# Decoder layer on one core: the last group's residual rows spaced, the order of two products in the gate and up blocks exchanged, and GpSimd's sums of weights held until the first group's residual is there

## The chip, the cores and the metric

The kernel runs on one core of one Trainium2 chip. The metric is the device time of one execution in microseconds (us). Of the kernel before, three runs gave 2595.02, 2599.94 and 2601.57 us; their median, 2599.94 us, is the time before.

## The reference

One layer of a hybrid decoder over 2048 tokens of 1024 numbers, in float32. The FFN is 2816 wide.

```python
a = _rmsnorm(h, g_pre_mix);  u = a @ w_in
conv_out = _conformer_conv(c_val, c_gate, ...)      # GLU, causal depthwise conv of width 31, LayerNorm, swish
attn_out = _rmsnorm(_stick_breaking(q, k, v), attn_norm_g)
y = concat([conv_out, attn_out]) @ w_out
h = h + _rmsnorm(y, g_post_mix)
f_in = _rmsnorm(h, g_pre_ffn)
f = (silu(f_in @ w_gate) * (f_in @ w_up)) @ w_down
h = h + _rmsnorm(f, g_post_ffn)
```

The attention has 8 heads of 64; for each query its weights are products of sigmoids that run backwards over the keys, so that a running product (a scan) stands where a softmax usually does.

## The kernel before, in words

The 2048 tokens are four groups of 512 (`NG`, `G`). Every float32 operand is split into a high part, rounded to TensorE's fp32r, and the low rest; a product is then three matmuls (high by low, high by high, low by high). ScalarE (ACT) writes the high part, VectorE (DVE) or GpSimd (POOL) subtracts to get the low one.

**Up to the last output projection** the order is set by a table, `PLAN` (L39): for each group the input projection ("in"), the convolution's and the attention's halves of the output projection ("outc", "outa"), then for groups 0 and 2 the first FFN products ("c11", "p4"). Three generators run beside it: `attn` (attention), `taps` (the convolution on DVE) and `sums` (L834). How far each may be advanced at a position of the table is a list of points: `ATTN`, `TAPS` and `SUMS` (L71: nothing before position 330, all by position 900). What these lists fix is the order in which the program is written. The framework then orders the instructions of each engine by readiness under a timeline of its own, so an instruction whose inputs and buffers are free can be placed far ahead of where it was written.

**The sums of weights.** The FFN products are done by a scheme of fast matrix multiplication on two by two blocks: it needs, besides the weights, sums and differences of their quarters. `sums` builds 132 of them on POOL (L844, `combine`), 88 from w_gate and w_up and 44 from w_down: each takes a load of 256 KB into one of three rotating tiles with the tag `sum`, one POOL operation on 128x512 numbers and a store of 256 KB (L772 for those of w_gate and w_up, two to a tensor, the pairs named (6, 5) and (7, 3); L766 for w_down). They are read again only in the FFN. In the attention POOL has other work: `om` (the running product, a DVE scan, L572) is multiplied into the weights `A` by POOL (L573), TensorE transposes `A` (L589, `at`), and goes on.

**The gate and up blocks** (`five`, L1106). After the last output projection there are 44 blocks: for the two FFN row groups g = 0 and g = 2 (each pairs two groups of 512 tokens), for each of 11 column blocks j, one block with the gate weights (i = 0) and one with the up weights (i = 1). A block is made of products numbered 3 to 7, of 12 matmuls each. Product 6 of the next block goes into a fresh bank `b2`; DVE reads it (`second`, L1131; u2 = b2 + s1); product 7 is added to the same bank and DVE reads that (u3 = b2 + s1); product 5 goes into a fresh bank `b3`, DVE adds it (u3 = b3 + u3), then product 3 is added to `b3` and read (b3 + u2). A product that adds to a bank has to wait until DVE has read what stood there. For g = 0 product 4 was computed earlier ("p4"), so a block is four products; for g = 2 it is five. The order of TensorE's products and of these DVE operations is pinned to the order of writing (`keep_in_program_order`). Per block TensorE runs product 5, product 7, product 6 of the next block, product 3. `hidden` (L1082) follows each up block: four DVE operations between tiles in on-chip memory (s1, s2, a difference, s4) make the operands of the down projection from the four results.

The operands of the blocks of g = 2 are themselves sums of quarters, made by `input_sums` (L886), which needs the normed residual rows of the last group. Those are made beside the first blocks: `steps` (L1197) takes `residual_parts` (L712) of four tiles of 128 rows, in two parts each, and then `input_sums`; one step is taken per block, or two in every second one from block 5 on (`todo`, L1216). A tile's residual is: a load of x, a square on ACT with a sum, a power on POOL (`rs`), a scaling on DVE (L722), two additions on POOL (L725), a store, a second square and power (`rstd2`), a scaling on ACT (L730). The load of x and the squares' output use tiles with the tag `row`, four of them, which the blocks use as well for their weights (`raw2`) and results (`a22`).

The splits of a block's weights into high and low parts are L1064 (ACT) and L1065 (POOL). After the blocks comes the down projection (`dps`).

## Time and profile before

The profiled execution of the kernel before took 2596.21 us by the device's clock; its span, from the first to the last instruction, is 2594.5 us.

| stretch of the span (us) | what runs | TensorE (PE) busy | DVE busy | POOL busy | GB/s |
|---|---|---|---|---|---|
| 0 to 430 | input projections, attention and convolution of the first groups | 388.41 | 327.25 | 281.86 | 297 |
| 430 to 1050 | the same of later groups, first FFN products | 576.07 | 532.90 | 399.95 | 305 |
| 1050 to 1450 | FFN products and attention of the last group | 392.38 | 248.87 | 197.16 | 237 |
| 1450 to 1542 | end of the attention, last output projection | 78.16 | 43.13 | 22.85 | 143 |
| 1542 to 1842 | gate and up blocks, g = 0 | 269.96 | 194.23 | 179.30 | 258 |
| 1842 to 2143 | gate and up blocks, g = 2 | 299.43 | 175.53 | 125.89 | 195 |
| 2143 to 2594 | down projection and the end | 430.18 | 266.72 | 266.10 | 214 |

A busy time is the time in which an engine has an instruction running, in this one execution; what is missing to the stretch's length is idle. GB/s is what all transfers moved. In rows of instructions, "out<-in" names tiles; the number behind the bar is the mean of one in ns; in rows of a timeline the square bracket gives the engine's idle time before the instruction and what ended it. In rows of waits the three numbers are the total in us, the count and the longest. Tiles of the blocks keep the names of the buffers that they reuse: u2 and u3 are written to `glu`, `cy` and `cs`; the operand of product 3 is `e__17579`, that of product 7 `e__17561`; `b` is a bank.

### The profile page before, as it was taken

What the parts mean: (1) busy time and instruction counts of PE and PEld (TensorE: products, weight loads), DVE (VectorE), ACT (ScalarE), POOL (GpSimd) and SP (SyncE); (2) the same over time, 40 slices, a digit from 0 to 9 for tenths busy, and PEclk for the clock granted to TensorE, in tenths of its full rate; (3) what the DMA queues carried; (4) which work ended last, traced back from release to release, by engine and by line L of the source; (5) the groups of instructions that cost most, each with busy time, mean ns of one, the idle gap of its engine ahead of it and who ended that gap; (6) DMA issues with size and microseconds to landing.
All of it is one profiled execution on the core that took longest, in us unless ns stands there. A gap on an engine that the chain in (4) does not pass through costs nothing. (4 is left out here: it accounts for less than half of the span.)

```text
span 2594.5 us, 35632 instructions
## 1 busy us (share of the span) xinstructions
PE 2434.6 (94%) x11156; PEld 1963.6 (76%) x11156; DVE 1788.6 (69%) x2321; ACT 1292.8 (50%) x2398; POOL 1473.1 (57%) x1844
## 2 busy tenths in 40 slices
PE   7989989998999999999999988899999999999997
PEld 6877767776777777887788766777777777887886
DVE  5797589958996898876544545766555655557556
ACT  4555555555555656667756734332332233453543
POOL 5764678556755777559433226764443444567556
PEclk9999999999999999999999989999999999999999
DMA  9989888988898898747977636986656557668655
GB/s 341 326 302 310 287 260 279 348 268 284 286 314 272 321 345 280 270 152 235 306 247 235 221 108 220 323 291 223 199 190 201 192 197 262 193 192 283 206 189 174
DMA packets 289182, 657.31 MB, mean 253 GB/s; under 512 B 33889, under 2 KB 42081, under 8 KB 288993
## 3 DMA queue, kind: packets, MB, share of 16 engines
q1 hardware_dynamic: 264704, 622.01, 71.6%
q10 hardware_dynamic: 24288, 33.04, 3.5%
q8 instruction: 88, 1.44, 0.2%
q14 instruction: 102, 0.83, 0.1%
HBM read 460.92 MB, written 193.99 MB: 252 GB/s over the span
## 5 line engine op out<-in xcount | busy, mean ns | idle before, releaser
L573 POOL TENSOR_TENSOR A<-A,om 128x512 f32<-128x512 f32 (+2 forms) x320 | 312.6, 977 | 410.0 <-DVE om L572 372.0
L572 DVE TENSOR_TENSOR_SCAN om<-om,one,z 128x513 f32<-128x513 f32 (+2 forms) x320 | 351.7, 1114 | 110.0 <-ACT A L570 104.5
L1065 POOL TENSOR_TENSOR wL<-raw,wH 128x512 fp32r<-128x512 f32 x176 | 248.9, 1441 | 286.5 <-issue 158.2
L476 DVE SCALAR_TENSOR_TENSOR cv<-glu,cw,cv 128x512 f32<-128x512 f32 x464 | 347.4, 749 | 6.7
L1245 DVE TENSOR_TENSOR xL__21999<-t__22001,xH__21998 128x512 fp32r<-128x512 f32 x154 | 199.1, 1301 | 159.6 <-ACT xH__21998 L1244 159.4
L1243 POOL TENSOR_TENSOR xL__21997<-t__22000,xH__21996 128x512 fp32r<-128x512 f32 x154 | 207.6, 1353 | 175.0 <-ACT xH__21996 L1242 174.5
L256 PE MATMUL inps<-xH,wL 128*128 128x512 f32 x640 | 260.8, 408 | 11.3 <-ACT sg L422 10.3
L249 DVE TENSOR_TENSOR TL<-at,TH 128x512 fp32r<-128x512 f32 (+1 forms) x320 | 188.8, 600 | 112.0 <-ACT TH L248 111.6
L260 PE MATMUL inps<-xL,wH 128*128 128x512 f32 x640 | 258.6, 405 | 0.2 <-DVE xL L392 0.2
L258 PE MATMUL inps<-xH,wH 128*128 128x512 f32 x640 | 258.2, 404 | 0.0
L760 PE MATMUL dps<-xH__21996,xL__21999 128*128 128x512 f32 x616 | 240.9, 391 | 8.1 <-DVE xL__21999 L1245 7.2
L568 ACT ACTIVATE om<-z 128x512 f32<-128x512 f32 (+2 forms) x320 | 171.6, 539 | 153.5 <-PE z L563 70.6
L760 PE MATMUL dps<-xL__21997,xH__21998 128*128 128x512 f32 x616 | 240.8, 391 | 2.0 <-POOL xL__21997 L1243 2.0
L760 PE MATMUL dps<-xH__21996,xH__21998 128*128 128x512 f32 x616 | 240.5, 390 | 0.0
L844 POOL TENSOR_TENSOR sum<-sum 128x512 f32<-128x512 f32 x132 | 172.6, 1308 | 84.8 <-DMA sum<-in_w_up_dram 28.5
L248 ACT ACTIVATE TH<-at 128x512 fp32r<-128x512 f32 (+1 forms) x320 | 168.0, 547 | 103.2 <-PE at L589 94.0
L1242 ACT ACTIVATE xH__21996<-t__22000 128x512 fp32r<-128x512 f32 x154 | 97.2, 631 | 233.0 <-POOL xL__21997 L1243 148.7
L589 PE MATMUL at<-idr,A 128*128 128x128 f32 x1088 | 191.4, 280 | 7.5 <-POOL A L573 5.6
L210 ACT ACTIVATE wH<-raw 128x1024 fp32r<-128x1024 f32 x156 | 165.6, 1064 | 65.0 <-DMA raw<-in_w_in_dram 29.6
L1064 ACT ACTIVATE wH<-raw 128x512 fp32r<-128x512 f32 x176 | 101.1, 623 | 165.0 <-PE b L760 76.4
L570 ACT ACTIVATE A<-z 128x512 f32<-128x512 f32 (+2 forms) x320 | 168.6, 542 | 19.2 <-PE at L589 14.4
L589 PEld LDWEIGHTS at<-idr,A 128*128 128x128 f32 x1088 | 142.2, 144 | 43.9 <-POOL A L573 6.8
(294 smaller groups left out, 6225.8 us busy)
## 6 DMA issues: line engine op xcount, KB each, us to landing
wL<-wL SPq DMA_DIRECT2D x156, 512.0 KB, 5.1
raw<-in_w_in_dram SPq DMA_DIRECT2D x80, 512.0 KB, 6.4
t__22001<-u SPq DMA_DIRECT2D x154, 256.0 KB, 2.8
c<-c ACTq DMA_DIRECT2D x88, 256.0 KB, 4.4
t__22000<-wd SPq DMA_DIRECT2D x88, 256.0 KB, 2.9
K<-kd SPq DMA_DIRECT2D x80, 256.0 KB, 4.7
V<-vd SPq DMA_DIRECT2D x80, 256.0 KB, 4.7
u<-accf SPq DMA_DIRECT2D x22, 768.0 KB, 4.1
```

Of the source, the lines that this page charges most:

```text
L249: nc.vector.tensor_tensor(L, ps, H.bitcast(F32), ALU.subtract)
L256: nc.tensor.matmul(ps, WL[:, kc], aH[t](k), start=k == 0, stop=False)
L258: nc.tensor.matmul(ps, WH[:, kc], aH[t](k), start=False, stop=False)
L260: nc.tensor.matmul(ps, WH[:, kc], aL[t](k), start=False, stop=k == KT - 1)
L476: nc.vector.scalar_tensor_tensor(to, gl[c][:, k:k + G], cw[:, c, k:k + 1], a, ALU.mult, ALU.add))
L572: nc.vector.tensor_tensor_scan(r, r, z[:, 0:1].to_broadcast([P, w + 1]), one, ALU.mult, ALU.bypass)
L573: nc.gpsimd.tensor_tensor(a[:, 0:w], a[:, 0:w], om[:, G - w + 1:G + 1], ALU.mult)
L589: nc.tensor.transpose(pt[:, j * P:(j + 1) * P], u["A"][j][:, b * P:(b + 1) * P], id32)
L760: return nc.tensor.matmul(ps, a, b, skip_group_check=True, **flags)
L1065: nc.gpsimd.tensor_tensor(l, t, f32(h), sub)
L1243: nc.gpsimd.tensor_tensor(WL, w, f32(WH), sub)
L1245: nc.vector.tensor_tensor(UL, t, f32(UH), sub)
```

## The change

**The sums of weights.** `SUMS` starts at position 414 of the table and ends at 930. In `sums`, three tiles with the tag `sum` are taken first and one number in each is set on POOL; then POOL adds to each a number of `rstd2[:, 3:4]`, which is made by the residual of the last tile of group 0. The real sums need the same three buffers, so none of their loads can be issued before that. The pairs stored together are now (6, 7) and (5, 3).

**The order of products.** Product 7 of a block now comes first and product 5 second. The second half of `hidden` is written between the two DVE operations on u3; its stores are queued in two portions.

**The residual of the last group.** The rows of x are loaded into four half tiles that are free at that time (`e[2:4]`), no longer into `row`; the squares' output goes to another small tile. A tile's residual has four parts instead of two, and the parts of a tile are written one block apart. `steps` has two steps more, and block 16 takes two.

```diff
-SUMS = ((330, 0.0), (900, 1.0))
+SUMS = ((414, 0.0), (415, 0.002), (930, 1.0))
...
-        r, junk = row("xr"), row("junk")
...
+        yield
         nc.sync.dma_start(hd[T], y)
         rms_of(rstd2[:, T:T + 1], y, junk)
         done.add(("h", T))
+        yield
...
+        held = [fup.tile([P, G], F32, tag="sum", name="held", bufs=3) for _ in range(3)]
+        for t in held:
+            nc.gpsimd.memset(t[:, 0:1], 0.0)
+        yield 0
+        for t in held:
+            nc.gpsimd.tensor_tensor(sp.tile([P, 1], F32, tag="held", name="h"), t[:, 0:1], rstd2[:, 3:4], add)
...
             dve(s1, a21, a22, add)
             dve(s2, s1, a11, sub)
+            for n, t in ((1, a11), (4, a22)):
+                late.append([1, t, "u", g, n, j])
+            yield
             dve(a21, a21, a11, sub)
             dve(s4, a12, s2, sub)
...
                 b3 = gu("b3")
-                b.mul(b3, 5, True)
+                b.mul(b.b2, 7, False)
                 nxt = Block(n + 1) if n + 1 < NB else None
                 for fn, *args in behind:
                     fn(*args)
                 c11 = result(b.i, (1, 1), b.c11)
-                b.mul(b.b2, 7, False)
+                b.mul(b3, 5, True)
                 u3 = next(u_)
                 dve(u3, b.b2, b.s1, add)
                 p4_ = b.A.get("p4")
                 if p4_ is not None:
                     dve(p4_, u3, p4_, add)
+                if more_h:
+                    next(more_h.pop())
                 dve(u3, b3, u3, add)
...
-            parts = [residual_parts((NG - 1) * TT + t, True) for t in range(TT)]
-            for t in range(TT + 1):
-                for p in parts[max(t - 1, 0):t + 1][::-1]:
+            xr = [m[:, i:i + 2, :].rearrange("p a t -> p (a t)") for m in operand(*e[2:4], dt=F32) for i in (0, 2)]
+            parts = [residual_parts((NG - 1) * TT + t, xr[t], keep=True) for t in range(TT)]
+            for t in range(TT + 3):
+                for p in parts[max(t - 3, 0):t + 1]:
                     next(p)
                 yield
...
-        todo = {n: [(next, more)] * (1 if n < 5 else 2 - n % 2) for n in range(16)}
+        todo = {n: [(next, more)] * (1 if n < 5 else 2 - n % 2) for n in range(17)}
```

POOL's order near the start of the program, before: `raw` and `wL` are weights of the first input projection, `sum` the sums of weights.

```order
L214 TENSOR_TENSOR wL_332<-raw_333,wH_331 128x1024
L844 TENSOR_TENSOR sum_5465<-sum_5463,sum_5465 128x512
L844 TENSOR_TENSOR sum_5463<-sum_5463,sum_5467 128x512
L844 TENSOR_TENSOR sum_5467<-sum_5465,sum_5467 128x512
L214 TENSOR_TENSOR wL_340<-raw_341,wH_339 128x1024
```

The first sums now, on the same engine, right behind the held tiles' additions and among the attention's operations (`A` is multiplied at L573, `rstd2` made at L192):

```order
L192 TENSOR_TENSOR rstd2_76<-ms_6498,nhalf_73 128x1
L192 TENSOR_TENSOR rstd1_75<-ms_7080,nhalf_73 128x1
L191 TENSOR_SCALAR ms_7188<-ss_7186 128x1
L848 TENSOR_TENSOR h_8140<-held_8134,rstd2_76 128x1
L848 TENSOR_TENSOR h_8142<-held_8135,rstd2_76 128x1
L192 TENSOR_TENSOR rstd1_75<-ms_7188,nhalf_73 128x1
L848 TENSOR_TENSOR h_8144<-held_8136,rstd2_76 128x1
L573 TENSOR_TENSOR A_4740<-A_4740,om_4737 128x512
```

The 132 sums have moved as a whole: before, the first stood ahead of POOL's first product `A` and the last behind the 208th of 320; now the first stands behind the 90th and the last behind the 298th, and 81 of them stand ahead of the 211th.

DVE's order at one gate block of g = 0 that follows an up block, before: from the read of product 3 (`b3` and u2) over the multiplication by the up result, the four operations of `hidden`, to the two reads of u3 with the addition to `a22` between them, and the read of the next product 6.

```order
L1072 TENSOR_TENSOR b3_18711<-b3_18711,cy_17518 128x512
L1072 TENSOR_TENSOR lng_117<-b3_18711,lng_117 128x512
L1072 TENSOR_TENSOR accf_17520<-lng_117,sumf_17523 128x512
L1072 TENSOR_TENSOR accf_17520<-accf_17520,sumf_17522 128x512
L1072 TENSOR_TENSOR lng_117<-lng_117,sumf_17522 128x512
L1072 TENSOR_TENSOR accf_17520<-sumf_17524,accf_17520 128x512
L1072 TENSOR_TENSOR cy_17518<-b2_18774,glu0_132 128x512
L1072 TENSOR_TENSOR a22_18726<-cy_17518,a22_18726 128x512
L1072 TENSOR_TENSOR cy_17518<-b3_18810,cy_17518 128x512
L1072 TENSOR_TENSOR cs_17519<-b2_18863,glu1_134 128x512
```

The same place now:

```order
L1080 TENSOR_TENSOR b3_18713<-b3_18713,cy_17530 128x512
L1080 TENSOR_TENSOR lng_117<-b3_18713,lng_117 128x512
L1080 TENSOR_TENSOR accf_17532<-lng_117,sumf_17535 128x512
L1080 TENSOR_TENSOR accf_17532<-accf_17532,sumf_17534 128x512
L1080 TENSOR_TENSOR cy_17530<-b2_18769,glu0_132 128x512
L1080 TENSOR_TENSOR a22_18728<-cy_17530,a22_18728 128x512
L1080 TENSOR_TENSOR lng_117<-lng_117,sumf_17534 128x512
L1080 TENSOR_TENSOR accf_17532<-sumf_17536,accf_17532 128x512
L1080 TENSOR_TENSOR cy_17530<-b3_18805,cy_17530 128x512
L1080 TENSOR_TENSOR cs_17531<-b2_18857,glu1_134 128x512
```

The first read of u3 and the addition to `a22` have moved ahead of the last two operations of `hidden`; the number of operations between the read of product 3 and the second read of u3 is the same.

DVE's order at the start of the blocks, before (`glu3` takes u2 of block 0, `cy` u3 of block 0):

```order
L1072 TENSOR_TENSOR glu3_138<-b2_17617,glu0_132 128x512
L1072 TENSOR_TENSOR cy_17518<-b2_17617,glu0_132 128x512
L1072 TENSOR_TENSOR a22_17597<-cy_17518,a22_17597 128x512
L1072 TENSOR_TENSOR cy_17518<-b3_17631,cy_17518 128x512
L1072 TENSOR_TENSOR cs_17519<-b2_17674,glu1_134 128x512
```

And now:

```order
L1080 TENSOR_TENSOR glu3_138<-b2_17629,glu0_132 128x512
L722 SCALAR_TENSOR_TENSOR big_17215<-big_17215,rs_17748,gain_17745 128x1024
L722 SCALAR_TENSOR_TENSOR big_17215<-big_17215,rs_17840,gain_17745 128x1024
L1080 TENSOR_TENSOR cy_17530<-b2_17629,glu0_132 128x512
L1080 TENSOR_TENSOR a22_17609<-cy_17530,a22_17609 128x512
L1080 TENSOR_TENSOR cy_17530<-b3_17643,cy_17530 128x512
L1080 TENSOR_TENSOR cs_17531<-b2_17686,glu1_134 128x512
```

The residual's scaling of tiles 0 and 1 (L722) has moved ahead of u3 of block 0; the scaling of tiles 2 and 3 stands between blocks 0 and 1, where before the four were spread up to block 4. So the order that the framework made draws the residual together, though it is written further apart. The transposes of the last group's rows, which begin after product 16 of the blocks before, begin after product 7.

More of the change, by code (lines that the diff above doesn't have):

```diff
@@ L705, in layer_kernel, with residual, residual_parts @@
     gpo = []
-    def residual(T, keep=False):
-        for _ in residual_parts(T, keep):
+    def residual(T):
+        for _ in residual_parts(T, row("xr"), row("junk")):
             pass
-    def residual_parts(T, keep):
+    def residual_parts(T, r, junk=None, keep=False):
         g, t = divmod(T, TT)
@@ L850, in flush @@
                 if kind == "S":
-                    ns = (6, 5) if m in (6, 5) else (7, 3)
+                    ns = (6, 7) if m in (6, 7) else (5, 3)
                     part(t, ns.index(m), 2, kind, *key, ns)
@@ L1050, in weights @@
             raws = []
-            for ns in ((6, 5), (7, 3)):
+            for ns in ((6, 7), (5, 3)):
                 r = wp.tile([P, D], F32, tag="raw", name="raw") if ns[0] == 6 else row("raw2")
@@ L1087, in hidden @@
             dve(s2, s1, a11, sub)
+            for n, t in ((1, a11), (4, a22)):
+                late.append([1, t, "u", g, n, j])
+            yield
             dve(a21, a21, a11, sub)
             dve(s4, a12, s2, sub)
-            for n, t in ((1, a11), (4, a22), (7, a21), (2, a12)):
+            for n, t in ((7, a21), (2, a12)):
                 late.append([1, t, "u", g, n, j])
             late.append([1, sums3, "u3", g, j])
+            yield
         late = []
@@ L1145, in five @@
             behind = []
+            more_h = []
             for n in range(NB):
                 b3 = gu("b3")
-                b.mul(b3, 5, True)
+                b.mul(b.b2, 7, False)
                 nxt = Block(n + 1) if n + 1 < NB else None
@@ L1183, in five @@
                 if b.i:
-                    behind.append((hidden, b.g, b.j))
+                    more_h.append(hidden(b.g, b.j))
+                    behind.append((next, more_h[0]))
                 behind += todo.get(n, ())
@@ L1188, in five @@
                 fn(*args)
+            next(more_h.pop())
             assert next(more, None) is None
```

## Prediction

> **What bounds the kernel now.** I read the page first, then the table of busy times by stretch, then TensorE's waits in the two stretches that the change touches, and last the instructions around single waits.
>
> From the page:
>
> ```profile
> span 2594.5 us, 35632 instructions
> PE 2434.6 (94%) x11156; PEld 1963.6 (76%) x11156; DVE 1788.6 (69%) x2321; ACT 1292.8 (50%) x2398; POOL 1473.1 (57%) x1844
> ```
>
> TensorE (PE) is busy 94% of the span, so what can be won is its idle time, 2594.5 - 2434.6 = 159.9 us, and what it loses by a lower clock. Where the idle time lies, by stretch:
>
> ```profile
> 0.00:430.00 430.00, 388.41 (x1856) 313.22 (x1857) 327.25 (x511) 228.44 (x437) 281.86 (x409) 0.98 0.89 297
> 430.00:1050.00 620.00, 576.07 (x2778) 464.83 (x2777) 532.90 (x754) 354.64 (x668) 399.95 (x603) 0.97 0.89 305
> 1050.00:1450.00 400.00, 392.38 (x1939) 320.30 (x1938) 248.87 (x325) 267.07 (x497) 197.16 (x357) 1.00 0.71 237
> 1542.00:1842.00 300.00, 269.96 (x1125) 213.04 (x1123) 194.23 (x231) 108.88 (x187) 179.30 (x138) 0.97 0.76 258
> ```
>
> PE is idle for 41.6, 43.9, 7.6 and 30.0 us in these four. The change takes sums of weights out of the first, puts them into the third, and rearranges the fourth.
>
> **The change, part by part. The sums of weights.** Where they run on POOL before:
>
> ```profile
> 0.00:430.00 430.00, 72.06 (x56) 0.98 0.89 297
> 430.00:1050.00 620.00, 100.55 (x77) 0.97 0.89 305
> ```
>
> By the order shown with the change, the first sum now comes behind POOL's 90th product A and 81 sums come ahead of the 211th. The trace has 79 products A in the first stretch, 211 by 1050 us:
>
> ```profile
> 0.00:430.00 430.00, 69.21 (x79) 0.98 0.89 297
> 430.00:1050.00 620.00, 130.78 (x132) 0.97 0.89 305
> ```
>
> So 56 sums leave the first stretch, the second keeps about as many (81 for 77), and 51 arrive in the third. POOL works in order, so a sum whose load has not landed holds up whatever stands behind it. One case, POOL and then PE:
>
> ```profile
> 341.65 2.62 POOL L844 TENSOR_TENSOR sum<-sum 128x512 f32<-128x512 f32 x2 [3.31 <-DMA sum<-in_w_gate_dram]
> ...
> 345.14 0.44 PE L589 MATMUL at<-idr,A 128*128 128x128 f32 x2 [3.65 <-POOL A L573]
> ```
>
> PE's waits for POOL in the first stretch, and for a transfer:
>
> ```profile
> PE at L589 <- POOL A L573: 5.3, 4, 3.6
> PE z L562 <- DMA K<-kd: 1.7, 1, 1.7
> PE cps L506 <- POOL cs L501: 1.6, 1, 1.6
> PE ops L690 <- POOL wL L214: 1.5, 1, 1.5
> ```
>
> 5.3 + 1.6 + 1.5 = 8.4 us. With the sums gone these can all go; behind them DVE is late next (327.25 of 430 us busy), so I take 6. In the third stretch the price is bounded by the stretch before it, where 77 sums run and PE waits for POOL this much, against the first stretch:
>
> ```profile
> PE c L760 <- POOL wL L214: 0.8, 1, 0.8
> PE at L589 <- POOL A L573: 0.3, 1, 0.3
> ```
>
> 1.1/77 x 51 = 0.7 us; at the rate of the first stretch 8.4/56 x 51 = 7.7 us. POOL there will have 197.16 + 51 x 1.31 (100.55/77) = 264 of 400 us, the share of the second stretch (400 of 620), so I take 1. The sums: -6 + 1 = **-5 us**, ends -8 and +7. The three additions to the held tiles read what POOL itself wrote; nothing waits longer for them. The sums' stores move too: they wait on SP's queue for POOL, with loads of keys and values behind them:
>
> ```profile
> SPq L772 <- POOL sum L844: 53.5, 39, 3.9
> ```
>
> I cost that at nothing, because those loads are issued ahead of their use and PE waited only 1.7 us for one; without that cover it is part of the third stretch's case below. The loads of x go to the same queue earlier, ahead of the blocks' weights, four of them, and have nothing to wait for.
>
> **The products of the blocks.** PE's matmuls in the fourth stretch by operand, the first of products 3 and 7:
>
> ```profile
> L760 PE MATMUL b<-e__17579,wL 128*128 128x512 f32 x88 | 38.6, 439 | 21.1 <-DVE cs L1072 8.1 <-DVE glu L1072 6.5 <-DVE cy L1072 6.5
> L760 PE MATMUL b<-e__17561,wL 128*128 128x512 f32 x88 | 35.6, 405 | 5.3 <-POOL wL L1065 3.9 <-DVE glu L1072 1.4
> ```
>
> All waits for DVE but one stand in front of product 3, 21.1 us in 13 waits. Four of them (3.5 us) are in up blocks, the first and the last:
>
> ```profile
> 1623.13 0.62 PE L760 MATMUL b<-e__17579,wL 128*128 128x512 f32 x1 [1.81 <-DVE cs L1072]
> ...
> 1830.55 0.50 PE L760 MATMUL b<-e__17579,wL 128*128 128x512 f32 x1 [0.98 <-DVE cy L1072]
> ```
>
> The other nine (17.6 us) are in gate blocks behind an up block, where the four operations of `hidden` precede both reads of u3. One of the nine, on DVE, POOL and PE:
>
> ```profile
> 1782.28 0.70 DVE L1072 TENSOR_TENSOR b<-b,cy 128x512 f32<-128x512 f32 x1 [0.85 <-PE b L760]
> ...
> 1786.51 1.77 DVE L1072 TENSOR_TENSOR lng<-lng,sumf 128x512 f32<-128x512 f32 x1
> 1788.20 1.77 DVE L1072 TENSOR_TENSOR accf<-sumf,accf 128x512 f32<-128x512 f32 x1
> 1789.90 0.68 DVE L1072 TENSOR_TENSOR cy<-b,glu 128x512 f32<-128x512 f32 x1
> 1791.02 0.69 DVE L1072 TENSOR_TENSOR a<-cy,a 128x512 f32<-128x512 f32 x1 [0.44 <-issue]
> 1791.75 0.69 DVE L1072 TENSOR_TENSOR cy<-b,cy 128x512 f32<-128x512 f32 x1
> ...
> 1783.04 6.39 POOL L1065 TENSOR_TENSOR wL<-raw,wH 128x512 fp32r<-128x512 f32 x4 [5.83 <-ACT wH L1064]
> ...
> 1792.49 0.50 PE L760 MATMUL b<-e__17579,wL 128*128 128x512 f32 x1 [1.89 <-DVE cy L1072]
> ```
>
> While POOL splits four halves of weights, an operation of DVE between two tiles in on-chip memory takes up to 1.77 us; those that read a bank take 0.68 to 0.70, and the same kind takes 0.69 once POOL is done (1791.02). The chain is nine operations, 10.2 us from 1782.28 to 1792.44; it starts when product 3 has ended and must end before the next product 3, with three products between (8.4 us, by the 2.79 below). The change leaves their number; it moves the first read of u3 and the addition to `a` between the two halves of `hidden`. The read of u3 (0.68) takes nothing from POOL, so POOL's third half goes by beside it and only one of the last two operations of `hidden` still meets POOL: 1.77 - 0.69 = 1.08 us less. I take 1.0 each, 9 us. Of the nine chains three hold two operations of `input_sums` more; of the new ones two, with three operations in all. Three operations of 0.7 us make 2 us. In up blocks u3 waited for product 7, one product before product 3; product 7 now ends one product earlier, and what remains is one read under product 6: all 3.5 us go. Reads -9 - 2 - 3.5 = -14.5.
>
> Behind some waits the matmuls are slow. The product behind the one of 1623.13, and another pair:
>
> ```profile
> 1627.58 0.39 PE L760 MATMUL b<-xH__17543,wL 128*128 128x512 f32 x1
> ...
> 1666.90 0.50 PE L760 MATMUL b<-e__17579,wL 128*128 128x512 f32 x1 [3.43 <-DVE cs L1072]
> 1671.34 0.40 PE L760 MATMUL b<-xH__17543,wL 128*128 128x512 f32 x1
> ```
>
> 12 matmuls took 4.45 and 4.44 us; undisturbed ones take 2.79 (1541.91 to 1544.70, below). That is 1.65 us each, and the stretch's granted clock is 0.97. Of five such places I let two and a half go: -4. The Trainium skill, page "TensorE: Matmul & The Clock Gate", section "Why this matters for your kernels", asks for no idle gaps over some 3 us. By that rule only the wait of 3.43 and one like it, of the five, would cost a slow product, and the term would be -3.3. The trace differs: the wait of 1.81 us has one too.
>
> At the start a cost comes in. The first products 6 and 5, and product 7 behind them:
>
> ```profile
> 1541.91 0.40 PE L760 MATMUL b<-xH__17525,wL 128*128 128x512 f32 x1
> 1544.70 0.40 PE L760 MATMUL b<-xH__17543,wL 128*128 128x512 f32 x1
> 1549.09 0.47 PE L760 MATMUL b<-e__17561,wL 128*128 128x512 f32 x1 [1.41 <-DVE glu L1072]
> ```
>
> Product 7 waits for DVE's read of product 6, which DVE reaches only at the end of a row of splits. Product 5 hid 2.79 us of that and now comes behind: +2.8, and with a slow product after so long a gap +1.6. In later blocks product 7 has product 3 as its cover, 2.79 us against one read of 0.68. The waits for POOL's splits (3.9 us) I leave: loads come earlier without x in `row`, but eight additions of the residual now stand together. The blocks: -14.5 - 4 + 4.4 = **-14 us**. Ends: all waits and slow products of this stretch gone (21.1 + 3.9 + 5 x 1.65 = 33), less 4.4, gives -29; nothing gained, +4.
>
> **Sum.** -5 - 14 = -19 us. The profiled execution took 2596.21 us, 1.7 more than its span; it would take 2577. The median of the three runs is 2599.94, 3.7 above the profiled one; on that scale the forecast is **2581 us**.
>
> **The rivals.** *DVE stays the bound in both places.* In the first stretch POOL's waits go over to DVE, and in the blocks the two scalings drawn ahead of the first u3 wait for their powers; before they waited so:
>
> ```profile
> L722 DVE SCALAR_TENSOR_TENSOR big<-big,rs,gain 128x1024 f32<-128x1024 f32 x4 | 5.1, 1284 | 19.3 <-POOL rs L192 19.3
> ```
>
> 19.3/4 = 4.8 us each; one of them in front of u3 costs that. Sums 0, blocks -14 + 4.8 + 1.6: -8, so 2592. For it speaks that the residual is drawn together and not spaced; against it that PE has two products left there.
>
> *The third stretch pays.* Its idle share becomes that of the second: 43.9/620 x 400 = 28 us for 7.6, +21. With -6 and -14 the time is 2600 + 1 = 2601. For it: POOL and transfers (237 + 51 x 0.52 MB / 400 us = 303 GB/s) reach the second stretch's level. Against: DVE, whose scans hold PE most in the second stretch, stays at 62%.
>
> *Slower: product 7 without its cover.* It now starts behind product 3, and u2 is read behind the second read of u3, which ended at 1792.44 in the chain above, with PE already waiting. Two `input_sums` operations or a scaling (1.3 us) in front of u2's read use up the 2.79 us. It decides from there on: 1.5 us more in each of the first eight blocks and a slow product in four, 12 + 6.6 = 18.6; with +4.4 at the start, half the gain of the later blocks (-7) and -5 for the sums, +11: 2611. For it: residual and transposes now fall into the first blocks (from product 7 on, not 16). Against it: in the order the operations stand mostly behind u2.
>
> *More: transfers set the pace at the start.* The sums in the first 100 us, with the share of the transfer engines (0.99) and GB/s:
>
> ```profile
> 0.00:100.00 100.00, 14.18 (x11) 0.98 0.99 344
> ```
>
> If nothing more fits in there, these 11 sums, each a load and a store of 128x512 numbers of 4 bytes (0.52 MB), cost 5.8 MB at 344 GB/s, 17 us, and the time is 2564. The Trainium skill, page "DMA: Bandwidth & Descriptors", section "Specifications", gives a core about 358 GB/s of HBM, which would say so. The trace speaks against it: PE waited for transfers 1.7 us in the whole first stretch.
>
> **How the numbers follow.** Forecast 0.62, DVE 0.13, third stretch 0.09, uncovered product 7 0.11, transfers 0.05. 0.3% of 2599.9 is 7.8 us, about what a measurement can tell from no change; faster is below 2592.1, slower above 2607.7. Faster: 0.62 + 0.05 + a quarter of the DVE case, 0.70; within: the rest of it and the third stretch, 0.19; slower 0.11. The range reaches down to 2562, past the transfers' case and near the sum of the good ends (-29 - 8), and up to 2604, past the third stretch's; it leaves out the slower case and a little of the rest. The first 1542 us are ordered anew as a whole, which moves single waits either way; the range holds that too.
>
> **What would show it.** Right: PE's idle time in the first stretch falls by some 6 us with no POOL wait behind a sum; the third stretch keeps under 10; the waits in front of product 3 fall from 21 to about 8 us, and a wait of some 4 us stands at the first product 7. Wrong: product 3 waits as before, or new waits at product 7 in many blocks, or the third stretch idle for 20 us.

## The result

Over six runs each the changed kernel took 2613.42 us (median), the kernel before 2600.76 us: ratio 1.0055, with a 95% interval of 1.0038 to 1.0073. By this ratio it is slower by 14 us where 19 us less were forecast, and it lies outside the range, beyond the upper end of 2604. The profiled execution took 2613.23 us.

From the page of the changed kernel:

```profile
span 2611.5 us, 35762 instructions
PE 2445.0 (94%) x11156; PEld 1965.5 (75%) x11156; DVE 1785.2 (68%) x2321; ACT 1287.6 (49%) x2398; POOL 1487.8 (57%) x1850
```

TensorE (PE) has the same 11156 instructions and is busy 10 us longer: the loss is idle time and slower matmuls, not work. The busy times by stretch; the fourth row is moved to where the blocks of g = 0 now stand:

```profile
0.00:430.00 430.00, 392.44 (x1868) 318.96 (x1869) 321.54 (x513) 226.43 (x438) 217.88 (x364) 0.97 0.71 231
430.00:1050.00 620.00, 566.13 (x2695) 451.01 (x2693) 515.08 (x731) 345.37 (x648) 393.70 (x587) 0.96 0.88 300
1050.00:1450.00 400.00, 379.09 (x1823) 302.90 (x1822) 249.93 (x325) 252.07 (x473) 264.39 (x405) 0.98 0.85 290
```
```profile
1575.90:1859.90 284.00, 265.05 (x1125) 209.28 (x1123) 206.47 (x231) 108.26 (x188) 191.57 (x140) 0.99 0.77 265
```

The blocks of g = 0 take 284 us for 300, as forecast. They begin at 1576 us for 1542: 34 us are lost ahead of them, in the part where only the sums of weights were changed. In the first stretch PE does 12 instructions more (1868 for 1856), in the second 83 fewer, in the third 116 fewer. The granted clock is lower in all three (0.97 for 0.98, 0.96 for 0.97, 0.98 for 1.00).

A fixed time is a poor ruler where work shifts. Below, stretches are cut by PE's own count of instructions (transposes included), which is the same up to the blocks in both kernels, 6900. By that count the changed kernel is 2 us ahead at the 1840th, and two pieces hold the loss. The first is from the 3910th to the 4140th, where the first FFN products begin beside the attention, before and after:

```profile
894.00:941.10 47.10, 45.49 (x232) 36.82 (x231) 45.70 (x65) 27.32 (x51) 34.83 (x43) 1.00 0.93 327
```
```profile
897.20:958.00 60.80, 52.83 (x232) 40.95 (x233) 54.46 (x75) 28.81 (x55) 34.75 (x45) 0.86 0.93 323
```

As many instructions take 13.7 us longer, 6.4 us of it idle time and 7.3 us slower matmuls, at a clock of 0.86 for 1.00. POOL is busy for the same time in both. The work is not quite the same: a comparison of PE's instructions shows 15 others in the changed kernel (14 of them transposes of `hrow`) in place of as many, mostly `c`, and DVE, busy 97% of the piece before, has ten operations and 8.8 us more. The second piece is from the 5060th to the 5980th, before and after:

```profile
1137.90:1330.20 192.30, 184.68 (x922) 149.34 (x921) 115.19 (x146) 132.31 (x250) 119.81 (x201) 1.00 0.75 248
```
```profile
1152.60:1367.80 215.20, 194.37 (x922) 151.46 (x921) 122.70 (x153) 134.72 (x257) 159.00 (x238) 0.97 0.82 279
```

22.9 us more, and here POOL has 39 us more work. What is left of the part ahead of the blocks adds up to -0.6: -2 + 13.7 + 22.9 - 0.6 = 34.

### The profile page after: what moved, and what is told of

The parts are those of the page before. It is cut to its first block, busy times and chain, and to the rows that moved or that the text cites. A ratio compares the mean times of both kernels' runs of the same rounds, so it can differ in the third digit from the quotient of the medians.

```text
span 2611.5 us, 35762 instructions
## 1 busy us (share of the span) xinstructions
PE 2445.0 (94%) x11156; PEld 1965.5 (75%) x11156; DVE 1785.2 (68%) x2321; ACT 1287.6 (49%) x2398; POOL 1487.8 (57%) x1850
## 4 chain that ended last, share of the span: by engine, by line
PE 61%; DVE 14%; DMA 12%; POOL 6%; issue 4%; ACT 2%; SPq 1%; ACTq 0%; POOLq 0%; DVEq 0%
PE b L762 16%; PE dps L762 13%; PE c L762 7%; DVE cv L476 4%; PE inps L256 3%; PE inps L258 3%; PE inps L260 3%; DVE om L572 3%; PE at L589 3%; PE z L562 2%; PE z L563 2%; PE o L595 1%; PE o L594 1%; DMA sum<-in_w_gate_dram 1%; PE ops L688 1%
## 5 line engine op out<-in xcount | busy, mean ns | idle before, releaser
L573 POOL TENSOR_TENSOR A<-A,om 128x512 f32<-128x512 f32 (+2 forms) x320 | 312.7, 977 | 379.7 <-DVE om L572 342.7
L1073 POOL TENSOR_TENSOR wL<-raw,wH 128x512 fp32r<-128x512 f32 x176 | 254.7, 1471 | 265.0 <-issue 164.5
L570 ACT ACTIVATE A<-z 128x512 f32<-128x512 f32 (+2 forms) x320 | 168.6, 543 | 21.9 <-PE at L589 16.4
```

The lines of the kernel that those rows point to most:

```text
L573: nc.gpsimd.tensor_tensor(a[:, 0:w], a[:, 0:w], om[:, G - w + 1:G + 1], ALU.mult)
L1073: nc.gpsimd.tensor_tensor(l, t, f32(h), sub)
```

## The experiments

Two theories stood against each other. H: the sums of weights cost where they now stand. R: the framework makes a new order for everything up to the blocks (below, a new draw) as soon as anything there is edited, and the order of before was one that any new draw loses. Before these two, the tail's part of the change (the order of products and the residual) was taken apart from the sums' part. Times in us that are compared between kernels are ratios to the kernel before, times 2600.

**The two parts apart.** `t_tail` is the changed kernel without its edits to the sums:

```diff
-SUMS = ((414, 0.0), (415, 0.002), (930, 1.0))
+SUMS = ((330, 0.0), (900, 1.0))
...
-        held = [fup.tile([P, G], F32, tag="sum", name="held", bufs=3) for _ in range(3)]
...
-            nc.gpsimd.tensor_tensor(sp.tile([P, 1], F32, tag="held", name="h"), t[:, 0:1], rstd2[:, 3:4], add)
```

> The changed kernel with the sums of weights put back as they were before (no held tiles, the old table), the order of products and the spaced residual kept. Theory H (the held sums cost the 34 us that the part up to the blocks lost, the blocks won their 17 us by themselves): 2600.8 - 17 = 2584 us, and the blocks begin at 1542 us of the span, as before. Rival R (the front is drawn anew by any edit, and the sums have no share in its loss): the blocks begin 15 us or more after 1542, and the time lies between 2598 and 2613 us.

Measured: 2578.6 us, ratio 0.9922 (0.9899 to 0.9944), faster than both kernels. Its blocks begin at 1546 us. PE's order up to the blocks is that of the kernel before, instruction by instruction: an edit of the tail alone draws nothing new there, against R as it is put above. `s_both` is the other half: the kernel before with the lines marked with a minus above.

> The kernel before with the held sums alone; blocks, residual and pairs as before. Theory H: the blocks begin 34 us later and gain nothing, 2600.8 + 30 to 34 = 2631 to 2635 us. Rival R: within 10 us of 2601 us. A third case, that both parts cost or gain only together (the blocks won because they began later), gives 2613 or less.

Measured: ratio 1.0100 (1.0075 to 1.0125), 26 us slower; the blocks begin at 1568 us and take 297. That is closer to H's 30 to 34 us than to R's 10 at most. So the two parts add up, -20 and +26 against +14, within 8 us, and the loss comes with the sums' edit. That does not yet say whether by their place or by the draw.

**The tail's two parts.** `t_order` is the kernel before with the order of products, the pairs and the split `hidden`; `t_resid` has only the residual in four parts:

```diff
+                b.mul(b.b2, 7, False)
...
+                b.mul(b3, 5, True)
```
```diff
...
+            xr = [m[:, i:i + 2, :].rearrange("p a t -> p (a t)") for m in operand(*e[2:4], dt=F32) for i in (0, 2)]
+            parts = [residual_parts((NG - 1) * TT + t, xr[t], keep=True) for t in range(TT)]
...
```

> The kernel before with the order of products and the two halves of the hidden sums changed, the residual of the last group and the sums of weights as before. If the order makes the gain of the blocks, as forecast (the waits in front of product 3 go from 21 to 8 us): 2582 to 2587 us beside 2597 of before. If the spaced residual makes most of it: 2590 or more. If product 7 misses its cover as long as the residual's operations are not moved: over 2597.

> The kernel before with the last group's residual in four parts, with its own places for x, alone; products, hidden sums and sums of weights as before. The order of products alone gave 0.997 (9 us of the 18 that both give). If the two parts add up: 9 us, 2590. If the residual helps only once product 7 stands first: 2597 to 2600. If it makes the waits for POOL's splits go (3.9 us in before) and no more: 2595.

Measured: 0.9970 (0.9956 to 0.9984) and 0.9975 (0.9963 to 0.9987), 8 and 6.5 us, together less than the 20 of both (and less than forecast for each, 10 to 15 and 9). The blocks take 291 and 294 us, and 279 with both, for 300.5 in the kernel before. The first of product 3 in the three, `t_order`, `t_resid`, `t_tail`, with its waits:

```profile
L760 PE MATMUL b<-e__17579,wL 128*128 128x512 f32 x88 | 37.0, 421 | 10.2 <-DVE glu L1072 5.4 <-DVE cy L1072 2.4 <-DVE cs L1072 2.3
```
```profile
L762 PE MATMUL b<-e__17579,wL 128*128 128x512 f32 x88 | 38.6, 439 | 22.4 <-DVE cs L1074 10.2 <-DVE cy L1074 7.1 <-DVE glu L1074 5.1
```
```profile
L762 PE MATMUL b<-e__17579,wL 128*128 128x512 f32 x88 | 35.6, 405 | 4.8 <-DVE cy L1074 2.9 <-DVE glu L1074 1.2 <-DVE cs L1074 0.6
```

The order of products takes the waits in front of product 3 away (21.1 to 10.2); the residual alone leaves them (22.4). What it takes away are waits for POOL's splits (3.9 to 0.6 us).

**POOL's work in the sums.** `a_nopool` leaves POOL's 132 operations out of the changed kernel, `a_short` cuts each to 8 of 512 numbers:

```diff
-            nc.gpsimd.tensor_tensor(c, a, b, op)
```
```diff
+            nc.gpsimd.tensor_tensor(c[:, 0:8], a[:, 0:8], b[:, 0:8], op)
```

> The changed kernel without POOL's 132 operations of the sums: each loaded quarter is stored as it came, so that loads, stores and the hold stay and the FFN gets other numbers. If the price lies in POOL's order (sums that wait for their load hold up the products A behind them): the waits of TensorE go, the blocks begin at 1545 us or earlier, 2580 us or less. If it lies in the transfers that now come later: as the changed kernel, 2605 to 2613 us.

> The changed kernel with each of POOL's sums cut to 8 of its 512 numbers a row, so that the FFN gets wrong sums; loads, stores, the hold and the wait of POOL for each load stay. Theory W (POOL's waits for the loads, with the products A queued behind them, are the price): near the changed kernel, 2600 us or more. Theory D (the 1.3 us that each sum works, and what it takes from DVE meanwhile, are the price): near the kernel without POOL's sums, 2575 us or less. Half and half: 2588.

Measured: 0.9877 (0.9851 to 0.9903), 46 us faster than the changed kernel, and 0.9957 (0.9940 to 0.9974), 25 us faster. So the transfers of the sums, which both keep, are not what costs. Each leaves out work and draws a new order too, so the totals say less than the pieces. From the 5060th to the 5980th instruction, first `a_nopool`, then `a_short`:

```profile
1137.60:1329.50 191.90, 184.81 (x922) 148.44 (x921) 120.97 (x155) 133.07 (x255) 118.76 (x202) 1.00 0.82 282
```
```profile
1134.30:1342.60 208.30, 191.34 (x923) 151.91 (x921) 119.29 (x149) 133.61 (x252) 128.78 (x235) 0.98 0.87 301
```

Without POOL's operations the piece is back at 191.9 us, though the transfers stay at 282 GB/s: its loss is POOL's. With short ones it keeps 16 of 23 us. There POOL stood idle for 14.9 us ahead of 30 sums, 9.8 of them by the row for loads; in the changed kernel 27 sums work 34.7 us there and wait 2.6:

```profile
L852 POOL TENSOR_TENSOR sum<-sum 128x512 f32<-128x512 f32 x27 | 34.7, 1286 | 2.6 <-DMA sum<-in_w_down_dram 2.3
```
```profile
L852 POOL TENSOR_TENSOR sum<-sum 128x8 f32<-128x8 f32 x30 | 6.5, 217 | 14.9 <-DMA sum<-in_w_down_dram 9.8 <-issue 4.9
```

So neither W nor D holds alone (the total fell on their middle, 2589). That the short sums cost by their wait is not shown: `a_short` is a new draw as well, and PE's largest new wait there is for the splits `wL` of POOL (6.4 us for 1.4). That the sums cost by slowing DVE meanwhile can be left aside: in the last three quarters of the piece a scan took 1.19 us on the mean in the changed kernel, for 1.18 before. The other piece, from the 3910th instruction, is no shorter without POOL's operations:

```profile
878.10:941.20 63.10, 52.15 (x233) 39.58 (x232) 51.44 (x70) 28.95 (x53) 30.75 (x43) 0.89 0.92 322
```

63.1 us, more than with the sums. That loss needs no work of the sums. The next two leave the operations of a part of the sums out, at their old place (`t_tail`):

```diff
+            made[0] += 1
+            if made[0] > 56:
+                nc.gpsimd.tensor_tensor(c, a, b, op)
```

and `made[0] <= 56` in the other.

> The kernel with the change's tail and the old place of the sums, without POOL's operation for the first 56 of the 132 sums, which are those of the first 430 us (their tensors get the quarters as loaded). If sums beside the first 430 us are as good as free, as the changed kernel's start says (2 us ahead at 400 us, for 56 sums less): 2574 to 2580 us. By the prediction's term for them (6 us): 2573. If a sum costs the same anywhere (45 us for 132, 0.34 each): 2560.

> The same kernel, without POOL's operation for the last 76 sums instead, those between 430 and 1050 us. If the price of a sum goes by its place (high once the first FFN products and the later groups' attention run): 2579 - 15 = 2564 us, more gained than with the first 56 left out. If the old place is free for all of them: within 5 us of 2579. If a sum costs the same anywhere: 2553.

Measured: 0.9997 (0.9987 to 1.0007) and 0.9908 (0.9896 to 0.9921). Against `t_tail`, leaving out the first 56 sums made the kernel 19.5 us slower, against all that was expected. Leaving out the last 76 gained 4 us, which is not clear of the noise, as the intervals overlap; it fits the case in which the old place is free. Less work cannot cost by itself: theory H has no room for the first, and R has.

**A new draw with next to nothing changed.** In `t_tail`, `n_first1` leaves out POOL's operation of one sum, the first, `n_mid1` that of the 60th (`if made[0] > 1:` and `if made[0] != 60:` in the lines above):

> The kernel with the change's tail and the old place of the sums, without POOL's operation for one single sum, the first of 132 (its tensor gets the quarter as loaded). That takes 1.3 us of work away in the first 20 us, and the framework draws a new order for the whole part up to the blocks: 2327 rows of TensorE's order differ, against 2765 between this kernel and the changed one. Theory R (the order of before is one that was found by trial, and any new draw loses most of what the held sums lost): 2590 to 2605 us. Theory H (the place of the sums is the price, a new draw alone costs nothing): 2576 to 2581 us.

> The same, without POOL's operation for the 60th sum alone, near 440 us: what comes before keeps its order, what comes behind is drawn anew (1654 rows of TensorE's order). Theory R: the stretches up to 430 us stay as they were, and 8 to 15 us are lost behind 1000 us, where the order of before leaves TensorE without a single gap: 2587 to 2594 us. Theory H: 2576 to 2581 us.

Measured: 0.9986 (0.9976 to 0.9997) and 0.9940 (0.9921 to 0.9960): 17 us lost by one operation of 1.3 us less, as R had it, and 5 us by one in the middle, between the two forecasts and not clear of the noise (`t_tail` reaches up to 0.9944). `n_attn` changes one number of a table of `t_tail`:

```diff
-ATTN = ((46, 0.0), (890, 1.0))
+ATTN = ((46, 0.0), (888, 1.0))
```

> The kernel with the change's tail, the old place of the sums, and one number of the table of the attention changed (its last point at position 888 for 890): no work added or taken, 1323 rows of TensorE's order differ, all in the later part. Ratio to before, 0.992 with the old number. R: what lies behind the first changed row loses 5 to 15 us, 0.994 to 0.998. H: 0.991 to 0.993.

Measured: 0.9942 (0.9926 to 0.9957), 5 us, again not clear of the noise, and just inside what R allowed.

**Holds by other events.** In the changed kernel, only the tile by which the sums are held was exchanged, as here in `a_hold3`:

```diff
-            nc.gpsimd.tensor_tensor(sp.tile([P, 1], F32, tag="held", name="h"), t[:, 0:1], rstd2[:, 3:4], add)
+            nc.gpsimd.tensor_tensor(sp.tile([P, 1], F32, tag="held", name="h"), t[:, 0:1], ma[0, 3][:, 0:1], add)
```

with `ma[0, 0]` in `a_hold0`, `rstd2[:, 0:1]`, `[:, 1:2]`, `[:, 2:3]` in `a_holdr0`, `h_r1`, `h_r2`, and `rstd1[:, 4:5]`, `[:, 7:8]` in `h_s4`, `h_s7`.

> The changed kernel with the sums held by an earlier event: they wait for a tile of group 0's attention output (its last pair of heads), not for the residual. In the order the first sum then stands near POOL's 40th product A, and 35 sums stand ahead of the 80th, where it was 0 with the residual and 56 without any hold. If the price grows with the number of sums displaced (21 of 56): about 2584 + 21/56 x 30 = 2595 us. If only sums behind 1050 us cost (here 93 stand ahead of the 160th product A, 113 without a hold, 56 in the changed kernel): 2584 + 20/57 x 30 = 2595 as well, and the third stretch tells, idle 12 of 400 us. If any hold costs by redrawing the front: 2605 or more. If the hold costs only past some point: 2584.

> The changed kernel with the sums held until the first pair of heads of group 0 is done, some 130 to 160 us: 43 sums ahead of the 80th product A (56 without a hold, 35 with the later hold that gave 1.0002, 0 in the changed kernel). If place and draw add up (draw 15 us, place 15 us by the share displaced, here 13 of 56): 0.992 + 0.006 + 0.0015 = 0.9995. If the draw is all: 0.994 to 1.003, and no order by place. If place is all: 0.995.

> The changed kernel with the sums held by the residual of group 0's first tile in place of its last: they begin a few us earlier, and all else is the same, but the order is drawn anew (2002 rows of TensorE's order differ from the changed kernel's). Theory H: 2609 to 2614 us, as the changed kernel. Theory R: anywhere between 2590 and 2620, and over 5 us from the changed kernel as likely as not.

> The changed kernel held by the residual of group 0's second tile in place of its last (the first gave 1.0012, the last 1.0055). The sums stand within 2 or 3 of the changed kernel's place. If late sums cost as such, beyond what any draw costs: all four of this kind lie above all draws with early sums, 1.000 to 1.006. If the draw is all: 0.994 to 1.006, with some of them under 0.9986.

> The same, held by the residual of the third tile. As for the second tile: 1.000 to 1.006 if late sums cost as such, and a spread down to 0.994 if the draw is all.

> The changed kernel with the sums held only until a scale of group 1's first rows is there, some 20 us into the span: 4 sums ahead of the first product A in place of 7, later ones at the old place or a few ahead; nothing left out. Ratio to the kernel before; 0.992 with the old draw, 0.9986 with the draw that lacks one sum, 1.0055 for the changed kernel. R (any new draw of the front costs 10 to 20 us, wherever the sums stand): 0.996 to 1.000. H (the place of the sums alone): 0.991 to 0.993.

> As the one before, held until the scale of group 1's last rows: 3 sums ahead of the first product A, and 4 or 5 behind the old place all along. R: 0.996 to 1.000. H: 0.992 to 0.994, by 5 of 56 sums displaced.

The three holds by the residual's other tiles took 11 to 16 us less than the changed kernel, one of them under 1.000, with the sums almost at the same place: the draw is part of its price. `h_s7` came out where H had it, `h_s4` above both ranges, `a_hold0` where draw and place can't be told apart (their sum, 0.9995, missed), and `a_hold3` between the forecasts. The totals alone decide little; the pieces say more.

All that ran, with the two pieces; the columns in us are worked out from the profiled execution as the time between the starts of those PE instructions. That is one execution of each kernel, and of some not a typical one (`h_s4`'s took 17 us less than its median, `n_attn`'s 9 us more). How far one execution can be trusted is seen where PE's order up to the blocks is the same: in before, `t_order`, `t_resid` and `t_tail`, and in after and `s_both`. Inside these two groups the pieces differ by up to 2.8 and 4.8 us, the start of the blocks by up to 8:

| kernel | sums | ratio to before (95%) | 3910th to 4140th | 5060th to 5980th | blocks begin |
|---|---|---|---|---|---|
| before | old place | 1 | 47.1 | 192.3 | 1542 |
| t_order | old | 0.9970 (0.9956 to 0.9984) | 48.4 | 193.8 | 1545 |
| t_resid | old | 0.9975 (0.9963 to 0.9987) | 47.7 | 191.4 | 1544 |
| t_tail | old | 0.9922 (0.9899 to 0.9944) | 47.2 | 192.0 | 1546 |
| n_mid1 | old, new draw behind 440 us | 0.9940 (0.9921 to 0.9960) | 53.0 | 191.0 | 1548 |
| n_attn | old, new draw of the later part | 0.9942 (0.9926 to 0.9957) | 57.8 | 193.5 | 1556 |
| h_s7 | early, new draw | 0.9926 (0.9909 to 0.9942) | 52.8 | 199.6 | 1542 |
| a_hold0 | a little later | 0.9945 (0.9928 to 0.9962) | 56.5 | 193.1 | 1536 |
| n_first1 | early, new draw | 0.9986 (0.9976 to 0.9997) | 56.6 | 194.2 | 1560 |
| h_s4 | early, new draw | 1.0029 (1.0006 to 1.0052) | 61.9 | 194.7 | 1563 |
| a_hold3 | between | 1.0002 (0.9988 to 1.0017) | 55.2 | 195.7 | 1566 |
| h_r2 | late | 0.9992 (0.9979 to 1.0006) | 59.1 | 205.5 | 1559 |
| a_holdr0 | late | 1.0012 (0.9998 to 1.0026) | 52.3 | 210.3 | 1571 |
| h_r1 | late | 1.0013 (1.0000 to 1.0025) | 57.4 | 210.9 | 1559 |
| after | late | 1.0055 (1.0038 to 1.0073) | 60.8 | 215.2 | 1576 |
| s_both | late | 1.0100 (1.0075 to 1.0125) | 58.0 | 210.4 | 1568 |
| a_short | late, cut to 8 numbers | 0.9957 (0.9940 to 0.9974) | 51.1 | 208.3 | 1555 |
| a_nopool | left out | 0.9877 (0.9851 to 0.9903) | 63.1 | 191.9 | 1534 |
| t_early0 | first 56 left out | 0.9997 (0.9987 to 1.0007) | 54.0 | 198.3 | 1557 |
| t_late0 | last 76 left out | 0.9908 (0.9896 to 0.9921) | 47.3 | 199.2 | 1537 |

Both theories hold in part, each in one piece. From the 5060th on, the place decides: 205.5 to 215.2 us in the five kernels with whole, late sums, 191 to 199.6 in the eleven with all or all but one of the sums early or between. From the 3910th on, the draw decides: 47 to 48 us in the four kernels with the order of before, 52 to 62 in every newly drawn one that has all or all but one of the sums, early (53 to 62) as late (52 to 61). `t_late0`, also a new draw from the 1984th instruction on, but with the last 76 sums left out, keeps 47.3.

In part this loss gives back what was gained just ahead of the piece: six of the twelve kernels drawn anew with all the sums or all but one (`n_attn`, `h_s7`, `a_hold0`, `h_s4`, `h_r1`, `h_r2`) come to the 3910th from the 3500th 5 to 8 us faster than before does. From the 3500th to the 4140th the twelve lie between 2 us ahead of before and 12 us behind it (the changed kernel 12 behind), the three with the order of before between 1 ahead and 2 behind. Elsewhere draws scatter both ways.

By the ratios, a new draw with early sums (`h_s7`, `a_hold0`, `n_first1`, `h_s4`) costs 1, 6, 17 and 28 us against `t_tail`, one with late sums 18, 23, 24 and 35: 13 and 25 on the mean, overlapping, so that on four draws each a difference of the totals isn't shown. In the piece from the 5060th on it is: the two groups don't overlap, and their distance (199.6 to 205.5) is above what one order differs by.

## Why the prediction was wrong, point by point

The step that failed is the price of the sums at their new place. The forecast took +1 us for the third stretch, by a bound read from PE's waits that name POOL; by PE's count that stretch lost 24.9 us. The second stretch, which had no term, lost 16.6 us. Against these 41.5 us stand smaller gains: 2.3 us in the first stretch (forecast 6), 5.3 from 1450 to 1542 us, for which there was no term either, 16.4 in the blocks (forecast 14) and 0.5 behind them. That leaves +17 us in the profiled executions.

**The first stretch: right mechanism, a third of the gain.** "With the sums gone these can all go; behind them DVE is late next, so I take 6." PE's waits in the first 430 us, after:

```profile
PE tps L266 <- DVE xrow L338: 8.4, 4, 7.4
PE z L562 <- DVE om L572: 7.5, 7, 2.2
PE inps L256 <- issue: 4.6, 1, 4.6
PE at L589 <- ACT ma L629: 4.2, 1, 4.2
PE o L595 <- DVE TL L249: 3.8, 4, 2.3
PE z L562 <- DMA QL<-qd: 3.6, 2, 1.8
```

All 8.4 us of waiting for POOL are gone, and new waits (an issue, ACT's `ma`, transfers of `QL`) stand there. Idle time fell by 4 us (41.6 to 37.6), the clock from 0.98 to 0.97, and PE is 2 us ahead at its 1840th instruction. What failed here is the word "can": the six waits did go, but the new order has waits of its own.

**The third stretch: the term was mis-sized.** "1.1/77 x 51 = 0.7 us", taken as 1, with 7.7 as the upper end; the piece from the 5060th on cost 22.9, and 13 to 23 in the five late kernels. POOL's load came as forecast (264.39 us busy for 264). But the bound was read from PE's waits that name POOL. The waits in that piece, before and then after, without those under 0.9 us:

```profile
PE z L562 <- DVE om L572: 3.9, 8, 0.7
PE o L595 <- DVE TL L249: 1.7, 2, 1.0
PE p L760 <- POOL wL L227: 1.4, 3, 0.5
```
```profile
PE z L562 <- DVE om L572: 9.6, 14, 2.8
PE o L594 <- ACT TH L248: 5.3, 6, 2.0
PE o L595 <- DVE TL L249: 1.6, 6, 0.4
PE p L762 <- POOL wL L227: 1.3, 2, 1.0
PE cps L506 <- POOL cs L501: 0.9, 1, 0.9
PE c L762 <- ACT c L803: 0.9, 1, 0.9
```

No wait for POOL's `A` stands there at all. The attention is a ring: scan (DVE), `A` (POOL), transposes (PE), `TH` (ACT), products (PE). What POOL holds up arrives at PE as a wait for ACT or DVE. The delay itself can be seen: worked out from the rows, a product `A` starts on the mean 0.94 us behind the end of its scan in this piece before, 1.61 after, and 0.81 without POOL's sums. All twenty traces agree on both. In the five late kernels this delay is 1.61 to 2.09 us, and PE waits 10.5 to 16.5 us for `om`, `TH` and `TL`; in the others the delay is 0.64 to 0.98 (`a_hold3`, between, 1.31) and those waits are 0.9 to 6.9 us. The delay tells the step and not its price: `h_r2` has the longest and loses least of the five. It is not what `a_short` loses by (delay 0.94, waits 6.7).

That POOL can hold up PE under another engine's name is seen well at 832 to 844 us of the changed kernel, ahead of both pieces. POOL, DVE and PE:

```profile
837.14 2.63 POOL L852 TENSOR_TENSOR sum<-sum 128x512 f32<-128x512 f32 x2 [3.28 <-issue]
839.73 1.09 POOL L573 TENSOR_TENSOR A<-A,om 128x512 f32<-128x512 f32 x1
...
841.43 0.55 POOL L192 TENSOR_TENSOR mv<-msc,nhalf 128x1 f32<-128x1 f32 x1
```
```profile
842.01 0.75 DVE L498 SCALAR_TENSOR_TENSOR cy<-cy,mv,lnb 128x512 f32<-128x512 f32 x1 [4.63 <-POOL mv L192]
...
843.01 0.68 DVE L611 TENSOR_REDUCE ot<-pf 128x256 f32<-128x512 f32 x1
```
```profile
843.75 0.47 PE L589 MATMUL at<-idr,A 128*128 128x128 f32 x1 [5.30 <-DVE ot L611]
```

Two sums keep POOL from 833.9 to 839.7 us, 3.28 of it idle, DVE idles 4.63 us behind POOL, PE 5.30 behind DVE, and PE's row names DVE. The rival that had this price, "the third stretch pays" (+21, chance 0.09), was right that this stretch pays, and near in size partly by luck: it had all of it as idle time (28 us), and idle time went from 7.6 to 20.9 us only, with the clock from 1.00 to 0.98 for the rest. Its total, 2601, had nothing for the second stretch.

**The second stretch: no term at all.** "The second keeps about as many (81 for 77)", so nothing was counted. It lost 17 us by PE's count, 13.7 of it in the piece that is longer in all twelve new draws with all the sums or all but one. The closing remark, that the first 1542 us are ordered anew and "the range holds that too", had the right risk and no number: the draws with all the sums and the new tail spread over 0.9926 to 1.0055, 34 us.

**The blocks: right.** Forecast -14, measured -16.4 in the changed kernel and -22 in `t_tail`. Its terms, from the first matmuls of product 3 and of product 7, after:

```profile
L762 PE MATMUL b<-e__17591,wL 128*128 128x512 f32 x88 | 36.6, 415 | 9.1 <-DVE glu L1080 5.0 <-DVE cy L1080 3.5 <-DVE cs L1080 0.6
L762 PE MATMUL b<-e__17573,wL 128*128 128x512 f32 x88 | 35.6, 405 | 4.2 <-POOL ms L191 4.2
```

The waits in front of product 3 fell from 21.1 to 9.1 us (forecast about 8). A wait of 4.17 us stands at the first product 7 for 1.41, +2.8 as forecast; the row names POOL's `ms`, but DVE's read of product 6 ended there, behind a row of splits:

```profile
1577.58 4.65 DVE L810 TENSOR_TENSOR e__17592<-sumin,e__17591 128x512 fp32r<-128x512 f32 x4 [0.83 <-ACT e__17591 L809]
1582.16 0.68 DVE L1080 TENSOR_TENSOR glu<-b,glu 128x512 f32<-128x512 f32 x1
```
```profile
1582.98 0.76 PE L762 MATMUL b<-e__17573,wL 128*128 128x512 f32 x1 [4.17 <-POOL ms L191]
...
1587.34 0.39 PE L762 MATMUL b<-xH__17555,wL 128*128 128x512 f32 x1
```

Product 7 took 4.36 us behind that wait, 1.57 more than 2.79 (forecast 1.6). Of the five slow products one is left, at 1646.63, behind a wait of 3.75 us, where the forecast let two and a half go; in these blocks both slow products followed waits of over 3.7 us. The shorter waits ahead of product 3, up to 1.6 us, had none behind them. Product 7 waits at no later block, so the rival that forecast 2611 by an uncovered product 7 did not happen, though the time came out near it.

**Transfers at the start.** In the first 100 us, where that rival saw 17 us to gain, the share of the transfer engines fell from 0.99 to 0.88 and PE did 368 instructions for 378; over the whole stretch the share fell from 0.89 to 0.71 and PE gained 2 us. Transfers did not set the pace there.

**What stays open.** Which interleaving makes the piece from the 3910th to the 4140th instruction take 47 to 48 us in the old order and, `t_late0` aside, 51 to 63 in new ones was not found. In it DVE is busy 45.7 of 47.1 us in the kernel before, and the waits that new draws show differ (`z`, `o`, the transposes of `hrow`). The twelve executions of `h_s4`, all in one order, spread over 31 us. They go with the granted clock, 0.98 at 2589 us and 0.97 at 2621; what sets it for one execution stays open, and so does how much of a draw's price is the clock's.

## What to carry to other kernels

Where a framework draws the order from readiness, an edit is two edits, the one meant and a new draw; price the second by a few edits that change next to nothing (one operation less, one number of a table) before reading a small result as the first. In a ring of engines, look for a slower engine in the delay of its own step and in the waits for every member of the ring, not only in the waits that name it. Try the parts of a change separately: here `t_tail`, 0.9922 (0.9899 to 0.9944), beats both kernels.

## What the runs showed of the hardware

Behind PE's first instruction, idle time ahead of the blocks grew by 16.5 us (99.7 to 116.2), 13 of it in waits under 3 us, and the same number of matmuls and transposes was busy another 17.4 us. That more waiting always costs as much again by slower matmuls does not follow: `t_order`, `t_resid` and `t_tail`, with PE's order of before, were idle 5 to 6 us less there than the kernel before and yet busy 7 to 10 us longer.

In the piece from the 3910th on, 8.0 us of idle time for 1.6, in waits of at most 1.56 us, came with a granted clock of 0.86 for 1.00. That mean is made of two stretches at half speed, the first behind 20 us in which PE was idle for 5.25:

```profile
900.15:910.39 10.24, 8.65 (x28) 6.42 (x27) 9.77 (x15) 3.68 (x6) 7.13 (x7) 0.50 1.05 354
927.46:934.29 6.83, 6.18 (x19) 4.73 (x20) 6.39 (x13) 4.67 (x9) 4.71 (x7) 0.50 0.67 229
880.00:900.00 20.00, 14.75 (x82) 10.49 (x81) 18.33 (x26) 15.55 (x32) 15.75 (x27) 1.00 0.93 323
```

So here waits that are each far under 3 us, close together, went with half speed.

In the blocks of g = 0 before, 21 operations of DVE read a bank while POOL split weights, and took 0.68 to 0.70 us, as others did without POOL. The 18 between tiles in on-chip memory took 1.07 to 1.78 us beside POOL, where 0.69 is the median without it. The read at 1789.90 us in the prediction could not show this, because POOL's splits had ended at 1789.43; the count over all blocks does.
